# A hybrid decoder layer: carried state and decayed inputs in three rounded passes, z for two token blocks at a time

## The chip, the cores and the metric

The kernel runs on one core of a Trainium2 chip. The metric is the device time of one execution in microseconds (us); a single run reports it, and several runs are summed up by their median. A profile is of one further execution. Engines are named as the profile names them: PE multiplies matrices (PEld is its weight load), DVE is the vector engine, ACT the scalar engine with the transcendental functions, POOL the general engine, SP the one that issues most transfers.

## The reference

One layer: a half-weighted SwiGLU feed-forward block, a mixer, and a second feed-forward block, each followed by a residual and a layer norm, on 512 tokens of 1024 channels. The mixer adds a sliding-window attention and a state-space branch. The change lies in the state-space branch, cut here to what it computes for each of 4 groups of 8 heads, in 4 chunks of 128 tokens:

```python
proj = h @ w_in                      # z, xbc, dt, gates are column ranges of proj
xbc = silu(causal_depthwise_conv(xbc, conv_w, conv_b))        # gives x, B, C
CB = einsum("bclgn,bcsgn->bcgls", Cc, Bc)
y_diag = einsum("bcgls,bcgkls,bcsgkp->bclgkp", CB, Lmat, xdt)  # Lmat = exp of decay sums
states = einsum("bclgn,bcgkl,bclgkp->bcgkpn", Bc, decay_states, xdt)
...
# step over the chunks: h = chunk_decay * h + states ; prev is h before the step
y_off = einsum("bclgn,bcgkpn,bcgkl->bclgkp", Cc, prev, exp(A_cum))
...
u = (y_diag + y_off + d_skip * x) * silu(z)
u = u * rsqrt(mean(u * u, per group) + eps) * norm_w           # then u @ w_ssm_branch
```

## The kernel before, in words

All matrices are fp32, and nearly every product is made in three rounded passes. A value is split into a rounded high half and the rest (both of the type F32R): ACT casts the high half, DVE subtracts it from the value. `mm3` (L123 to L126) then issues high x high, high x rest and rest x high into one accumulator, as three matmuls with 512 moving columns (rows at L124, L125, L126). Weights come as 512 KB transfers on SP's queue into one of 3 `raw` buffers and are split by `split_w` into `wh` (ACT, L99) and `wl` (DVE, L100), 4 buffers each. Activations are split by `split_act` (ACT copy, then the DVE subtraction at L145). Two products of the state-space branch are not split but plain fp32 matmuls: `po`, C times the carried state `prev` (L615), and `pst`, B times the decayed inputs `xds` (L621). An fp32 matmul shows as two records, so that each line has 24 records for its 12 products.

The generator `ssd(g)` does one group. For a chunk c, `lead` lets POOL make four `ud` (L572); `decays` has PE sum them (L583, L584), ACT take exp of that (`seg`), DVE multiply `seg` twice by `cb`, itself from a PSUM product (L591, L593), DVE make `xdt` (L595) and POOL make `yx` (L597) and `xds` (L601). `products` has PE multiply `seg` by `xdt` (L609, 8 small products, 16 records), then `po` and `pst`; DVE adds these up into `yx`; POOL scales `prev` (L626), DVE adds `pst` to it. DVE then multiplies `yx` by `zs`, ACT takes the sum of squares, DVE scales it (`rs`, L633), POOL raises it to -1/2 (`rs`, L634), and DVE multiplies `yx` by it (L635). `turn(c)` has PE transpose the finished `yx` (L642, 4 blocks) for the next product. So from the end of a chunk's products to its `turn` there is a chain DVE, ACT, DVE, POOL, DVE, PE.

`weave` runs ssd(g), in ten steps, between large products ("mains"). First z of group 0, the convolution tiles (`xbc`) of group 1 and z of group 1 run beside ssd(0), whose ten steps fall on eight of the sixteen mains; then w_ssm of group 0 with the tiles and z of group 2 beside ssd(1); the same one further beside ssd(2); then w_ssm of group 2 and eight `gs_tile` beside ssd(3). In the profile ssd(0) takes about 621 to 723 us, ssd(1) 723 to 830, ssd(2) 830 to 918, ssd(3) 918 to 1027. `z_tiles` computes z of a group in four parts: each part loads one weight tile and multiplies it with all four token blocks, in four accumulators. A `gs_tile` makes a gate: a tanh to `tg`, a transfer of `tg` out and of `m1` in (POOL's queue), and two DVE operations on `ysum`.

The Tile framework places the instructions of this program on the engines; each engine then runs its own list strictly in that order, and waits at an instruction whose inputs or buffer are not there. PSUM has 8 banks here, 4 called `acc` for the large products and 4 called `sm` for the small ones.

Of the kernel before, what the change touches and what calls it, by code (L numbers as in the profile page):

```python
# [9 lines left out]
F32 = mybir.dt.float32  # L10
F32R = mybir.dt.float32r
# [3 lines left out]
P = 128  # L15
# [24 lines left out]
def hybrid_layer(  # L40
# [15 lines left out]
    def acc(name="acc"):  # L56
        return psum.tile([P, 512], F32, tag="acc", name=name)
# [230 lines left out]
    with tc.tile_pool(name="mix", bufs=1) as mix:  # L288
# [41 lines left out]
        def z_tiles(g, pool):  # L330

            pss = []

            def part(k2):
                if k2 == 0:
                    pss.extend(acc("z") for _ in range(NT))
                w2 = load_w(wcols(w_in, k2 * 256, 2, OFF_Z + g * 512, 512))
                for t in range(NT):
                    tok = slice(t * P, (t + 1) * P)
                    for j in range(2):  # L340
                        k = 2 * k2 + j
                        mm3(pss[t], xT[:, k, 0, tok], xT[:, k, 1, tok], w2[0][:, j], w2[1][:, j], k == 0, k == 7)
                if k2 < 3:
                    return
                for t in range(NT):
                    zs = pool.tile([P, 512], F32, name="zs", bufs=4)
                    nc.scalar.activation(zs, pss[t], AF.Tanh, scale=0.5)
                    nc.vector.scalar_tensor_tensor(zs, zs, 1.0, pss[t], ALU.add, ALU.mult)
                    cst["z", g, t] = zs

            return [lambda k2=k2: part(k2) for k2 in range(4)]
# [195 lines left out]
        with tc.tile_pool(name="ssd", bufs=1) as sp:  # L547
            ysum = sp.tile([P, 8, SEQ], F32, name="ysum")

            def ssd(g):  # L550
# [13 lines left out]
                st = [{} for _ in range(NT)]  # L564

# [11 lines left out]
                def decays(c):  # L577
# [20 lines left out]
                    xds = None  # L598
                    if c + 1 < NT:
                        xds = sp.tile([P, 512], F32, name="xds", bufs=1)  # L600
                        nc.gpsimd.tensor_tensor(hv(xds), hv(xdt), hb(dec[:, 1, c, hs]), ALU.mult)  # L601
                    st[c].update(segs=segs, xdt=xdt, yx=yx, xds=xds)

                def products(c):
# [7 lines left out]
                    if c > 0:  # L612
                        prev = st[c]["prev"]
                        po = sm()
                        nc.tensor.matmul(po, CT[:, tok], prev, start=True, stop=True)  # L615
# [3 lines left out]
                    if c + 1 < NT:  # L619
                        pst = sm()  # L620
                        nc.tensor.matmul(pst, Bn[:, c], xds, start=True, stop=True)  # L621
                        new = sp.tile([P, 512], F32, name="prev", bufs=2)
                        if c == 0:
                            nc.vector.tensor_copy(new, pst)
# [112 lines left out]
```

## Time and profile before

| quantity | value |
| --- | --- |
| time, median of 3 runs | 1453.4 us (1451.15 to 1454.14) |
| time of the profiled execution | 1453.2 us |
| span of the profiled execution | 1451.5 us |
| busy PE / DVE / ACT / POOL | 98% / 55% / 33% / 13% |
| granted PE clock, mean | 0.994 |

The span runs from the first to the last instruction that the profiler saw; 1.7 us of the execution lie around it. A busy share tells how long an engine had work in it. An engine that is busy nearly all the time is where the time is spent, unless its work is itself held up inside.

### The profile page before, as it was taken

Reading aid. Unit: us, or ns where it says so; the run is one execution under the profiler, and the core shown is the slowest. Engines: PE = TensorE matmul, PEld = TensorE weight load, DVE = VectorE, ACT = ScalarE, POOL = GpSimd, SP = SyncE. Lnnn points to the kernel's source line nnn. Section 1 sums busy time; section 2 is a strip of 40 time slices with the busy share of each in tenths; the row PEclk is TensorE's granted clock in tenths of the full one; section 3 lists DMA queues with packets and bytes.
Section 4 is the critical chain, followed back from the end, with each engine's and each line's share of the span. In section 5 each row is a group of like instructions: output and inputs, shape, how many; then the busy total and the mean of one; then the engine's idle time right before and its main releaser. Section 6 shows DMA issues by size and latency. Waiting matters only on the chain. (4 is left out here: it accounts for less than half of the span.)

```text
span 1451.5 us, 17121 instructions
## 1 busy us (share of the span) xinstructions
PE 1426.5 (98%) x6700; PEld 1169.7 (81%) x6700; DVE 791.5 (55%) x1246; ACT 482.1 (33%) x789; POOL 195.3 (13%) x214
## 2 busy tenths in 40 slices
PE   8999999999999999999999999999999999999997
PEld 6888888888877777887888888878878888888885
DVE  4343343233867884358659588686574434433235
ACT  4232232121346775223444234223313322322220
POOL 1000000000000000245244154261110000000001
PEclk9999999999999999999999999999999999999999
DMA  8433333323422133641231322345735333333321
GB/s 273 121 88 102 98 90 102 99 89 105 138 81 72 45 86 108 199 119 56 80 87 59 95 73 74 95 124 161 222 110 181 95 102 95 95 102 93 97 87 58
DMA packets 195633, 154.46 MB, mean 106 GB/s; under 512 B 6532, under 2 KB 169424, under 8 KB 195552
## 3 DMA queue, kind: packets, MB, share of 16 engines
q1 hardware_dynamic: 188608, 130.17, 30.1%
q0 software_dynamic: 6944, 23.19, 5.0%
q8 instruction: 53, 0.87, 0.3%
q14 instruction: 28, 0.23, 0.0%
HBM read 140.76 MB, written 12.58 MB: 106 GB/s over the span
## 5 line engine op out<-in xcount | busy, mean ns | idle before, releaser
L100 DVE TENSOR_TENSOR wl<-raw,wh 128x1024 fp32r<-128x1024 f32 (+1 forms) x233 | 299.6, 1287 | 417.3 <-ACT wh L99 412.6
L99 ACT CAST wh<-raw 128x1024 fp32r<-128x1024 f32 (+1 forms) x233 | 244.3, 1050 | 694.4 <-issue 323.7
L124 PE MATMUL acc<-xT,wh 128*128 128x512 f32 (+2 forms) x1120 | 441.9, 395 | 0.0
L125 PE MATMUL acc<-xT,wh 128*128 128x512 f32 (+2 forms) x1120 | 434.8, 388 | 0.0
L126 PE MATMUL acc<-xT,wl 128*128 128x512 f32 (+2 forms) x1120 | 433.8, 387 | 0.0
L124 PEld LDWEIGHTS acc<-xT,wh 128*128 128x128 f32 x1120 | 210.9, 188 | 44.5 <-issue 3.2
L125 PEld LDWEIGHTS acc<-xT,wh 128*128 128x128 f32 x1120 | 210.7, 188 | 44.2 <-issue 3.3
L126 PEld LDWEIGHTS acc<-xT,wl 128*128 128x128 f32 x1120 | 210.4, 188 | 43.0 <-issue 0.2
L124 PE MATMUL dn<-wh,hT 128*128 128x512 f32 x352 | 137.2, 390 | 0.0
L125 PE MATMUL dn<-wl,hT 128*128 128x512 f32 x352 | 137.1, 390 | 0.0
L126 PE MATMUL dn<-wh,hT 128*128 128x512 f32 x352 | 136.9, 389 | 0.0
L160 POOL TENSOR_TENSOR sts<-sts,cols 128x1 f32<-128x1 f32 x12 | 11.9, 990 | 719.9 <-DVE sts L159 719.9
L572 POOL TENSOR_TENSOR ud<-upper,dAr 128x512 fp32r<-128x512 f32 x64 | 86.4, 1378 | 104.2 <-PE sm L584 104.2
L239 DVE TENSOR_TENSOR t<-t,acc 128x512 f32<-128x512 f32 x44 | 30.2, 687 | 111.6 <-PE acc L126 111.4
L125 PEld LDWEIGHTS dn<-wl,hT 128*128 128x128 f32 x352 | 66.1, 188 | 13.7
L126 PEld LDWEIGHTS dn<-wh,hT 128*128 128x128 f32 x352 | 66.1, 188 | 13.6
L124 PEld LDWEIGHTS dn<-wh,hT 128*128 128x128 f32 x352 | 66.1, 188 | 13.6
L124 PE MATMUL z<-wh,xT 128*128 128x512 f32 x128 | 51.5, 402 | 0.0
L124 PE MATMUL acc<-uT,wh 128*128 128x512 f32 x128 | 50.5, 395 | 0.0
L126 PE MATMUL z<-wh,xT 128*128 128x512 f32 x128 | 49.9, 390 | 0.0
L125 PE MATMUL z<-wl,xT 128*128 128x512 f32 x128 | 49.9, 390 | 0.0
L126 PE MATMUL acc<-uT,wl 128*128 128x512 f32 x128 | 49.9, 390 | 0.0
(212 smaller groups left out, 1691.8 us busy)
## 6 DMA issues: line engine op xcount, KB each, us to landing
raw<-in_w_in_dram SPq DMA_DIRECT2D x66, 512.0 KB, 3.7
raw<-in_ffn_w_gate_dram SPq DMA_DIRECT2D x44, 512.0 KB, 3.8
raw<-in_ffn_w_up_dram SPq DMA_DIRECT2D x44, 512.0 KB, 3.7
raw<-in_ffn_w_down_dram SPq DMA_DIRECT2D x44, 512.0 KB, 3.6
raw<-in_w_ssm_branch_dram SPq DMA_DIRECT2D x16, 512.0 KB, 3.4
raw<-in_w_attn_branch_dram SPq DMA_DIRECT2D x8, 512.0 KB, 4.1
raw<-in_w_out_dram SPq DMA_DIRECT2D x8, 512.0 KB, 4.4
r<-in_x_dram SPq DMA_DIRECT2D x8, 256.0 KB, 5.7
```

The lines of the kernel that those rows point to most:

```text
L99: nc.scalar.copy(h[:, :n], raw[:, :n])
L100: nc.vector.tensor_tensor(l[:, :n], raw[:, :n], f(h[:, :n]), ALU.subtract)
L124: nc.tensor.matmul(ps, lh, rh, start=start, stop=False)
L125: nc.tensor.matmul(ps, lh, rl, start=False, stop=False)
L126: cur["mm"] = nc.tensor.matmul(ps, ll, rh, start=False, stop=stop)
L160: nc.gpsimd.tensor_tensor(mv[:, 3:4], mv[:, 2:3], mhalf[:, 0:1], ALU.pow)
L239: nc.vector.tensor_tensor(t, t, pu, ALU.mult)
L572: nc.gpsimd.tensor_tensor(ud[:, i], upper.unsqueeze(1).broadcast_to([P, 4, P]), f(dAr[:, i, c, h0:h0 + 4]).unsqueeze(2).broadcast_to([P, 4 ...
```

## The change

Three things change. First, `po` and `pst` go through `mm3`. Their operands are split by `split_act` into new tiles: `csp` (of C, 128 x 128) and `prs` (of `prev`, 128 x 512) for chunks 1 to 3, `bsp` (of B, 128 x 128) and `xds` (128 x 512, from POOL's product, now called `xd`) for chunks 0 to 2. All have one buffer. That makes 48 new ACT copies and 48 new DVE subtractions in all. `prev` is kept in one buffer and updated in place, so that POOL may scale it only after its split has been made. Second, `z_tiles` computes two token blocks at a time: parts 0 and 1 load two weight tiles each and do the first two blocks, parts 2 and 3 load none and do the other two with the same four tiles; two accumulators are in use at a time, and tanh and the DVE operation on the first two blocks come after part 1. Third, the `tg` and `m1` tiles of `gs_tile` are taken from the pools of `th` (2 buffers) and `ct` (3 buffers) instead of tiles with one buffer each.

```diff
--- before.py
+++ after.py
@@ -329,26 +329,28 @@
 
         def z_tiles(g, pool):
 
-            pss = []
-
-            def part(k2):
-                if k2 == 0:
-                    pss.extend(acc("z") for _ in range(NT))
-                w2 = load_w(wcols(w_in, k2 * 256, 2, OFF_Z + g * 512, 512))
-                for t in range(NT):
-                    tok = slice(t * P, (t + 1) * P)
-                    for j in range(2):
-                        k = 2 * k2 + j
-                        mm3(pss[t], xT[:, k, 0, tok], xT[:, k, 1, tok], w2[0][:, j], w2[1][:, j], k == 0, k == 7)
-                if k2 < 3:
+            ws, pss = [], []
+
+            def part(i):
+                pair, half = divmod(i, 2)
+                if pair == 0:
+                    ws.extend(load_w(wcols(w_in, k2 * 256, 2, OFF_Z + g * 512, 512)) for k2 in (2 * half, 2 * half + 1))
+                if half == 0:
+                    pss[:] = [acc("z") for _ in range(2)]
+                for k2 in (2 * half, 2 * half + 1):
+                    for j, ps in enumerate(pss):
+                        tok = slice((2 * pair + j) * P, (2 * pair + j + 1) * P)
+                        for k in (2 * k2, 2 * k2 + 1):
+                            mm3(ps, xT[:, k, 0, tok], xT[:, k, 1, tok], ws[k2][0][:, k % 2], ws[k2][1][:, k % 2], k == 0, k == 7)
+                if half == 0:
                     return
-                for t in range(NT):
+                for j, ps in enumerate(pss):
                     zs = pool.tile([P, 512], F32, name="zs", bufs=4)
-                    nc.scalar.activation(zs, pss[t], AF.Tanh, scale=0.5)
-                    nc.vector.scalar_tensor_tensor(zs, zs, 1.0, pss[t], ALU.add, ALU.mult)
-                    cst["z", g, t] = zs
-
-            return [lambda k2=k2: part(k2) for k2 in range(4)]
+                    nc.scalar.activation(zs, ps, AF.Tanh, scale=0.5)
+                    nc.vector.scalar_tensor_tensor(zs, zs, 1.0, ps, ALU.add, ALU.mult)
+                    cst["z", g, 2 * pair + j] = zs
+
+            return [lambda i=i: part(i) for i in range(4)]
 
         def xbc(g, pool):
             order = [4 * g + i for i in range(4)] + [16 + g, 20 + g]
@@ -562,6 +564,7 @@
                     return ap.rearrange("p (h d) -> p h d", h=HPG)
 
                 st = [{} for _ in range(NT)]
+                prev = []
 
                 def lead(c):
                     st[c]["ud"] = []
@@ -596,9 +599,18 @@
                     yx = sp.tile([P, 512], F32, name="yx", bufs=2)
                     nc.gpsimd.tensor_tensor(hv(yx), hv(xn[:, c]), hb(dB[:, hs]), ALU.mult)
                     xds = None
+                    if c > 0:
+                        csp = sp.tile([P, 2, P], F32R, name="csp", bufs=1)
+                        split_act((csp[:, 0], csp[:, 1]), CT[:, tok])
+                        st[c]["csp"] = csp
                     if c + 1 < NT:
-                        xds = sp.tile([P, 512], F32, name="xds", bufs=1)
-                        nc.gpsimd.tensor_tensor(hv(xds), hv(xdt), hb(dec[:, 1, c, hs]), ALU.mult)
+                        xd = sp.tile([P, 512], F32, name="xd", bufs=1)
+                        nc.gpsimd.tensor_tensor(hv(xd), hv(xdt), hb(dec[:, 1, c, hs]), ALU.mult)
+                        bsp = sp.tile([P, 2, P], F32R, name="bsp", bufs=1)
+                        split_act((bsp[:, 0], bsp[:, 1]), Bn[:, c])
+                        xds = sp.tile([P, 2, 512], F32R, name="xds", bufs=1)
+                        split_act((xds[:, 0], xds[:, 1]), xd)
+                        st[c]["bsp"] = bsp
                     st[c].update(segs=segs, xdt=xdt, yx=yx, xds=xds)
 
                 def products(c):
@@ -610,22 +622,25 @@
                                          start=True, stop=True)
                     nc.vector.tensor_tensor(yx, yx, py, ALU.add)
                     if c > 0:
-                        prev = st[c]["prev"]
+                        prs, csp = st[c]["prs"], st[c]["csp"]
                         po = sm()
-                        nc.tensor.matmul(po, CT[:, tok], prev, start=True, stop=True)
+                        mm3(po, csp[:, 0], csp[:, 1], prs[:, 0], prs[:, 1], True, True)
                         yo = sp.tile([P, 512], F32, name="yo", bufs=1)
                         nc.vector.tensor_tensor(hv(yo), hv(po), hb(dec[:, 0, c, hs]), ALU.mult)
                         nc.vector.tensor_tensor(yx, yx, yo, ALU.add)
                     if c + 1 < NT:
+                        bsp = st[c]["bsp"]
                         pst = sm()
-                        nc.tensor.matmul(pst, Bn[:, c], xds, start=True, stop=True)
-                        new = sp.tile([P, 512], F32, name="prev", bufs=2)
+                        mm3(pst, bsp[:, 0], bsp[:, 1], xds[:, 0], xds[:, 1], True, True)
                         if c == 0:
-                            nc.vector.tensor_copy(new, pst)
+                            prev.append(sp.tile([P, 512], F32, name="prev", bufs=1))
+                            nc.vector.tensor_copy(prev[0], pst)
                         else:
-                            nc.gpsimd.tensor_tensor(hv(new), hv(prev), hb(dec[:, 2, c, hs]), ALU.mult)
-                            nc.vector.tensor_tensor(new, new, pst, ALU.add)
-                        st[c + 1]["prev"] = new
+                            nc.gpsimd.tensor_tensor(hv(prev[0]), hv(prev[0]), hb(dec[:, 2, c, hs]), ALU.mult)
+                            nc.vector.tensor_tensor(prev[0], prev[0], pst, ALU.add)
+                        prs = sp.tile([P, 2, 512], F32R, name="prs", bufs=1)
+                        split_act((prs[:, 0], prs[:, 1]), prev[0])
+                        st[c + 1]["prs"] = prs
                     nc.vector.tensor_tensor(yx, yx, cst.pop(("z", g, c)), ALU.mult)
                     rs = sp.tile([P, P], F32, name="rs", bufs=2)
                     sq = sp.tile([P, 512], F32, name="yo", bufs=1)
@@ -673,10 +688,10 @@
 
             def gs_tile(j):
                 ps = gemm_T(load_w(wcols(w_in, 0, 8, OFF_GS + j * P, P)), xT, range(8))
-                tg = sp.tile([P, SEQ], F32, name="tg", bufs=1)
+                tg = mix.tile([P, SEQ], F32, name="th", bufs=2)
                 nc.scalar.activation(tg, ps, AF.Tanh, scale=0.5)
                 nc.gpsimd.dma_start(gsd[j], tg)
-                m1 = sp.tile([P, SEQ], F32, name="m1", bufs=1)
+                m1 = mix.tile([P, SEQ], F32, name="ct", bufs=3)
                 nc.gpsimd.dma_start(m1, m1d[j])
                 nc.vector.scalar_tensor_tensor(ysum[:, j], tg, 1.0, ysum[:, j], ALU.add, ALU.mult)
                 nc.vector.tensor_tensor(ysum[:, j], ysum[:, j], m1, ALU.add)
```

The framework's lists change with it. The lines of the kernel after are some 2 to 15 higher: L572 is L575, L597 is L600, L601 is L608 (`xds` is `xd`), L626 is L639, L634 is L649, L635 is L650.

On POOL, in the last two chunks of group 0: the `rs` (L634) of its second, third and fourth chunk (the only three `rs` here), among the `ud` of its own fourth chunk (the first `ud` row) and the `ud`, `yx` and `xds` of group 1. Before:

```order
L572 TENSOR_TENSOR ud<-upper,dAr 128x512 x4
L634 TENSOR_TENSOR rs<-rs,cols 128x1
L597 TENSOR_TENSOR yx<-xn,heads 128x512
L634 TENSOR_TENSOR rs<-rs,cols 128x1
L572 TENSOR_TENSOR ud<-upper,dAr 128x512 x4
L597 TENSOR_TENSOR yx<-xn,heads 128x512
L601 TENSOR_TENSOR xds<-xdt,dec 128x512
L634 TENSOR_TENSOR rs<-rs,cols 128x1
```

After:

```order
L575 TENSOR_TENSOR ud<-upper,dAr 128x512
L639 TENSOR_TENSOR prev<-prev,dec 128x512
L575 TENSOR_TENSOR ud<-upper,dAr 128x512 x3
L649 TENSOR_TENSOR rs<-rs,cols 128x1
L600 TENSOR_TENSOR yx<-xn,heads 128x512
L575 TENSOR_TENSOR ud<-upper,dAr 128x512 x4
L649 TENSOR_TENSOR rs<-rs,cols 128x1
L600 TENSOR_TENSOR yx<-xn,heads 128x512
L608 TENSOR_TENSOR xd<-xdt,dec 128x512 x2
L649 TENSOR_TENSOR rs<-rs,cols 128x1
```

The first `rs` still stands behind the fourth chunk's four `ud`, and now behind the scaling of `prev` of the chunk after its own as well; the second moved from before group 1's four `ud` to behind them; the last stood behind one `xds` of group 1 and stands behind two `xd`.

On POOL, from the fourth chunk of group 1 to its end. Before:

```order
L572 TENSOR_TENSOR ud<-upper,dAr 128x512 x4
L597 TENSOR_TENSOR yx<-xn,heads 128x512
L634 TENSOR_TENSOR rs<-rs,cols 128x1
L572 TENSOR_TENSOR ud<-upper,dAr 128x512 x4
L601 TENSOR_TENSOR xds<-xdt,dec 128x512
L597 TENSOR_TENSOR yx<-xn,heads 128x512
L634 TENSOR_TENSOR rs<-rs,cols 128x1
```

After:

```order
L575 TENSOR_TENSOR ud<-upper,dAr 128x512 x4
L600 TENSOR_TENSOR yx<-xn,heads 128x512
L575 TENSOR_TENSOR ud<-upper,dAr 128x512 x3
L649 TENSOR_TENSOR rs<-rs,cols 128x1
L575 TENSOR_TENSOR ud<-upper,dAr 128x512
L608 TENSOR_TENSOR xd<-xdt,dec 128x512
L600 TENSOR_TENSOR yx<-xn,heads 128x512
L608 TENSOR_TENSOR xd<-xdt,dec 128x512
L649 TENSOR_TENSOR rs<-rs,cols 128x1
```

The `rs` of the third chunk (the first here) moved from before the next group's `ud` to behind three of them, and a second `xd` came ahead of the last `rs`. Group 2 reads alike, with two `ud` in place of three.

On DVE, in the third chunk of group 3, from the product with `zs` of the second chunk to the `seg` products. Before:

```order
L629 TENSOR_TENSOR yx<-yx,zs 128x512
L633 TENSOR_SCALAR rs<-rs 128x1
L635 SCALAR_TENSOR_TENSOR yx<-yx,rs,normB 128x512
L100 TENSOR_TENSOR wl<-raw,wh 128x1024
L681 SCALAR_TENSOR_TENSOR ysum<-tg,ysum 128x512
L591 TENSOR_TENSOR cb<-sm,quarter 128x128
L682 TENSOR_TENSOR ysum<-ysum,m_7427 128x512
L593 TENSOR_TENSOR seg<-seg,cb 128x512 x2
```

After (the lines 644, 648, 650, 594 and 596 are the 629, 633, 635, 591 and 593 of before):

```order
L145 TENSOR_TENSOR prs<-prev,prs 128x512
L644 TENSOR_TENSOR yx<-yx,zs 128x512
L145 TENSOR_TENSOR bsp<-Bn,bsp 128x128
L145 TENSOR_TENSOR xds<-xd,xds 128x512
L598 TENSOR_TENSOR xdt<-xn,dth 128x512
L648 TENSOR_SCALAR rs<-rs 128x1
L696 SCALAR_TENSOR_TENSOR ysum<-th,ysum 128x512
L594 TENSOR_TENSOR cb<-sm,quarter 128x128
L650 SCALAR_TENSOR_TENSOR yx<-yx,rs,normB 128x512
L697 TENSOR_TENSOR ysum<-ysum,ct 128x512
L596 TENSOR_TENSOR seg<-seg,cb 128x512 x2
L100 TENSOR_TENSOR wl<-raw,wh 128x1024 x2
```

Four subtractions come in ahead of the `seg` products, and the weight split that stood ahead of them stands behind them.

## Rows read from the trace of the kernel before

**Rows 1.** Page, busy time of each engine (us, share of the span, instructions)

```profile
PE 1426.5 (98%) x6700; PEld 1169.7 (81%) x6700; DVE 791.5 (55%) x1246; ACT 482.1 (33%) x789; POOL 195.3 (13%) x214
```

**Rows 2.** Groups by line and shape, PE (busy us, mean ns | idle before)

```profile
L615 PE MATMUL sm<-prev,CT 128*128 128x512 f32 x24 | 14.5, 689 | 0.0
```

**Rows 3.** Timeline of PE, group 1, chunk 2 (start, us, instruction)

```profile
785.95 1.08 PE L615 MATMUL sm<-prev,CT 128*128 128x512 f32 x2
786.87 1.02 PE L621 MATMUL sm<-xds,Bn 128*128 128x512 f32 x2
787.32 0.79 PE L124 MATMUL acc<-xT,wh 128*128 128x512 f32 x1
787.95 0.40 PE L125 MATMUL acc<-xT,wh 128*128 128x512 f32 x1
```

**Rows 4.** Windows (us, then busy PE, PEld, DVE, ACT, POOL; clock; DMA share; GB/s)

```profile
620.80:723.00 102.20, 99.88 (x472) 80.44 (x471) 73.10 (x93) 37.52 (x58) 43.86 (x40) 0.98 0.28 82
...
680.10:683.40 3.30, 3.30 (x8) 1.50 (x6) 3.30 (x5) 1.58 (x3) 0.00 (x0) 0.50 0.24 68
...
970.30:973.60 3.30, 3.30 (x6) 1.40 (x5) 3.30 (x6) 0.00 (x0) 0.62 (x2) 0.50 0.76 255
```

**Rows 5.** Timeline of PE, rows with a wait (in brackets: idle before, releaser)

```profile
662.79 1.10 PE L609 MATMUL sm<-xdt,seg 128*128 128x64 f32 x8 [0.80 <-DVE seg L593]
...
677.78 1.10 PE L609 MATMUL sm<-xdt,seg 128*128 128x64 f32 x8 [0.54 <-DVE seg L593]
...
679.22 0.99 PE L609 MATMUL sm<-xdt,seg 128*128 128x64 f32 x7 [0.34 <-DVE seg L593]
...
709.40 0.63 PE L642 MATMUL sm<-ident,yx 128*128 128x128 f32 x4 [0.64 <-DVE yx L635]
...
968.09 2.00 PE L609 MATMUL sm<-xdt,seg 128*128 128x64 f32 x16 [1.16 <-DVE seg L593]
```

**Rows 6.** Groups by line and shape, DVE (busy us, mean ns | idle)

```profile
L145 DVE TENSOR_TENSOR hT<-t,hT 128x512 fp32r<-128x512 f32 x44 | 30.1, 685 | 0.0
...
L591 DVE TENSOR_TENSOR cb<-sm,quarter 128x128 f32<-128x128 f32 x16 | 4.5, 279 | 0.0
```

**Rows 7.** Timeline of POOL, groups 0 and 1

```profile
652.04 1.04 POOL L601 TENSOR_TENSOR xds<-xdt,dec 128x512 f32<-128x512 f32 x1 [3.87 <-PE sm L621]
...
670.09 5.08 POOL L572 TENSOR_TENSOR ud<-upper,dAr 128x512 fp32r<-128x512 f32 x4 [0.95 <-PE sm L584]
...
792.99 0.55 POOL L634 TENSOR_TENSOR rs<-rs,cols 128x1 f32<-128x1 f32 x1 [6.47 <-DVE rs L633]
794.37 4.93 POOL L572 TENSOR_TENSOR ud<-upper,dAr 128x512 fp32r<-128x512 f32 x4 [0.84 <-PE sm L584]
801.67 2.02 POOL L601 TENSOR_TENSOR xds<-xdt,dec 128x512 f32<-128x512 f32 x1 [2.36 <-DVE xdt L595]
```

**Rows 8.** Timeline of DVE, groups 0, 1 and 3

```profile
697.24 1.23 DVE L100 TENSOR_TENSOR wl<-raw,wh 128x1024 fp32r<-128x1024 f32 x1 [0.36 <-ACT wh L99]
...
796.88 0.74 DVE L305 SCALAR_TENSOR_TENSOR CT<-acc,cols,CT 128x509 f32<-128x509 f32 x1
...
808.29 0.75 DVE L635 SCALAR_TENSOR_TENSOR yx<-yx,rs,normB 128x512 f32<-128x512 f32 x1 [0.66 <-POOL rs L634]
...
962.48 2.06 DVE L100 TENSOR_TENSOR wl<-raw,wh 128x1024 fp32r<-128x1024 f32 x1
...
967.36 1.28 DVE L593 TENSOR_TENSOR seg<-seg,cb 128x512 f32<-128x512 f32 x2
```

**Rows 9.** Timeline of PE, group 1, chunk 3 and its end

```profile
801.16 1.90 PE L609 MATMUL sm<-xdt,seg 128*128 128x64 f32 x16
...
804.28 0.40 PE L126 MATMUL z<-wh,xT 128*128 128x512 f32 x1
...
809.07 0.40 PE L126 MATMUL z<-wh,xT 128*128 128x512 f32 x1
809.30 0.60 PE L642 MATMUL sm<-ident,yx 128*128 128x128 f32 x4
```

## The prediction

> **What bounds the kernel now.** First the busy time: PE works in 1426.5 of 1451.5 us [rows 1], so only work taken from PE, or a wait of PE taken away or put in, changes the time. Then the groups by line: the two plain fp32 products are 24 in all, with 24 records each [rows 2]. Then PE's own rows with a wait, in the stretch of the state-space branch (621 to 1027 us): they are few, between 0.3 and 1.2 us, and all come from DVE's `seg` or from the finished `yx` [rows 5]. Before PE's rows, last, the rows of POOL and DVE that feed them. The windows show two more losses there: 3.3 us at half clock in group 0 and again in group 3, right behind a wait, each of which does the work of half its length, so some 1.7 us are lost [rows 4].
>
> **The products.** The rounded passes start 21 passes apart at 804.28 and 809.07: 4.79 / 21 = 0.228 us each [rows 9]. A `po` and a `pst` next to each other start at 785.95, and the second rounded pass behind them at 787.95 [rows 3]. One pass taken off, two fp32 products take 787.95 - 0.23 - 785.95 = 1.77 us, 0.89 each. Three passes take 0.68, so 0.21 less; 24 products give **-5.0 us**. The first pass behind an fp32 product starts late (787.32 to 787.95 is 0.63 for one pass), and I count that as the fp32 product's cost. If it were not the product's but came with any change of operand, a new product would pay it again, and next to nothing would be won: the bounds of the term are -5.0 and 0. I take -5.0, since the passes of large products follow each other at 0.23 also where every pass loads other weights, as it would here.
>
> **The new splits.** 48 ACT copies lie on an engine that is busy 37.52 of 102.20 us in group 0 [rows 4] and cost nothing there by themselves. Of the 48 DVE subtractions, 24 are long, 0.69 us as the subtraction of the same shape in the feed-forward block, and 24 short, 0.28 as the 128 x 128 product [rows 6]: 23 us over four groups, 5.8 in each. DVE is busy 73.10 of 102.20 in group 0 [rows 4], so they fit into it; the time hangs on where they and the lists put the chain behind `seg` and `yx`. I go through the places where PE waits, or has little in hand.
>
> Group 3, chunk 2. PE waits 1.16 for `seg` at 968.09 [rows 5] because a weight split of 2.06 stands ahead of the `seg` products on DVE [rows 8]; the list after has it behind them. The new subtractions are ahead of them too, but they can run while DVE would wait for `rs`. I take the whole wait and half clock as gone: 1.3 (the wait and the lost start) + 1.7 = **-3.0**. If the half clock comes anyway it is -1.3.
>
> Group 0, chunk 1: the wait of 0.80 at 662.79 [rows 5] goes, since a weight split and an `xdt` leave the place ahead of `seg`, some 2.6, against 1.7 of new subtractions: **-0.8**.
>
> Group 0, chunk 2: the `rs` of chunk 1 stands behind four `ud` of 5.08 [rows 7], and now behind the scaling of `prev` too, a POOL product of the shape that takes 1.04 to 2.02 [rows 7]. So `turn` waits 1.2; the 0.54 at 677.78 and 0.34 at 679.22 [rows 5] go, since the first `seg` is now ahead of the last `yx` product: **+0.3**. The half clock there (680.1) I keep as it is.
>
> Group 0, chunk 3: `rs` of chunk 2 moves behind four `ud` (4.93 for four in group 1 [rows 7]) that themselves wait until PE has read the ones of chunk 3. DVE's `yx` product, and behind it `cb` and `seg`, wait as long. Before, there were some 4 us in hand: **+1.2**, with 0 to 2.5 as bounds.
>
> End of group 0: PE waits 0.64 already [rows 5]. The last `rs` now stands behind two `xd`; the second of them waits until the first has been split, 1.5 for the second `xd` and that split; a third weight split, 1.23 when alone [rows 8], stands ahead on DVE. Against that PE has 45 passes from `po` to `turn` in place of 39, 6 x 0.23 = 1.4. So 0.64 + 1.5 + 1.2 - 1.4 = 2.0, and **+1.5** with the 0.2 that PE comes earlier (the shorter `po`). Bounds 0 and 2.7, the latter if the 1.4 does not count.
>
> Group 1, chunk 3: `rs` of chunk 2, at 792.99 before the `ud`, moves behind three of them, which start at about 794.2 [rows 7]: 794.2 + 3 x 1.23 + 0.55 = 798.4, and with the `yx` product of 0.75, two operations of 0.74 and two `seg` of 0.64 each [rows 8] behind it the second `seg` is ready at 798.5 + 0.75 + 1.5 + 1.3 = 802.0, some 0.1 later with hand-overs. PE starts its products at 801.16 [rows 9], earlier in the changed kernel by what was won till then in this chunk, 0.4, and needs the second `seg` at half of them, 801.6: **+0.5**, and 0.3 more for two restarts, **+0.8**. Group 2 has two `ud` there and so 1.2 in hand: nothing.
>
> Ends of groups 1 and 2: `yx` is ready at 808.29 + 0.75 = 809.04 [rows 8], PE comes to `turn` at 809.30 [rows 9]: 0.26 in hand. Now `yx` waits for `rs` behind a second `xd`, which waits for an `xdt`, which on DVE stands behind the product of `yx` and `zs`: 0.2 + 0.6 later, if the `xd` takes 1.04, and 1.0 more if it takes 2.02 [rows 7]; PE comes 0.2 earlier. 0.8 + 0.2 - 0.26 = 0.74 each: **+1.5**.
>
> **The other two edits.** `z_tiles` issues the same passes from the same loads in the same order of transfers, and the four `zs` come two by two; four weight buffers are held longer, so the next load's split waits longer, but two raw tiles can lie ready. I count nothing; the bound is one late weight split per group, 1.2 x 4 = +5. The buffers of `gs_tile` give room in group 3 alone, where PE's one wait has been counted: nothing.
>
> **The sum.** -5.0 - 3.0 - 0.8 + 0.3 + 1.2 + 1.5 + 0.8 + 1.5 = -3.5. The profiled execution took 1453.2 us, 1.7 more than its span and 0.2 less than the median of the runs shown: 1449.7, and by the median some 0.2 more. I say **1449.8**.
>
> **Rivals.** *Nothing new waits.* The positive terms, 5.3 in all, stay out because POOL and DVE reach those steps earlier than I put them: 1449.8 - 5.3 = 1444.5. For it speaks that each is only 0.3 to 1.5 on chains of 5 to 10 us; against it that PE has only 0.26 in hand at two group ends and nothing at the third.
>
> *The passes win nothing* (the bound above): 1449.8 + 5.0 = 1454.8. For it, the 0.63 of the first pass after the fp32 products; against it, that no such step shows between large passes.
>
> *More half clock.* A wait of over 1 us was followed by half clock in group 3, and one of 0.54 and 0.34 in group 0 [rows 4, 5]. If two of the new waits bring one each, of 1.7: 1453.2.
>
> *DVE and POOL in each other's way: slower.* A weight split takes 2.06 in one place and 1.23 in another [rows 8], and POOL's `xds` 2.02 and 1.04 [rows 7]: the long ones lie beside work of the other engine, 0.8 to 1.0 extra each. The change puts 24 long subtractions on DVE, each with both its inputs in SBUF. If, at the six places with a wait above, both long subtractions (`prs` and `xds`) meet a POOL product, 12 x 0.9 = 10.8 more lie on the path: 1460.6. It is slower than before by over 2.9 from seven of the twelve on (7 x 0.9 = 6.3). For it, that POOL is busy 43.86 of 102.20 [rows 4], so four in ten would meet one by chance, which is five of the twelve; against it, that the subtractions wait for POOL's own `xd` and so start when it has ended. The Trainium skill, page "SBUF — State Buffer", section "Who interferes with whom", says that a DVE instruction with two SBUF inputs contends with a GpSimd instruction that reads SBUF, and that the one that comes second is held up for the whole of the other. The trace agrees with it in kind: 0.83 on a split and 0.98 on an `xds`, not whole instructions of the other. By the whole of the other, 1.23 for each `ud`, the rival would cost 12 x 1.23 = 14.8 instead.
>
> **Chances and range.** The forecast 0.42, its own range 1447.5 to 1452; nothing new waits 0.20; passes win nothing 0.08; more half clock 0.16; slower 0.14. What a measurement of this kernel can tell is about 0.2%, 2.9 us: faster is below 1450.5, slower above 1456.3. Faster takes all of the second and somewhat over half of the forecast's 0.42 (0.26), and little else: 0.47. Slower is the last rival, 0.14; the rest, 0.39, is the same. The range reaches from 1444.3, the case in which nothing waits, to 1456.0, which holds the two middle rivals and leaves the slower one out.
>
> **What would show it.** Right: in the profile after, `po` and `pst` are three records each, 0.23 apart, also from the last one to the next large product; the half clock at the third chunk of group 3 is gone and no wait for `seg` stands there; at the three `turn`s that end groups 0 to 2, PE waits for `yx` for 0.7 to 2 us, with `rs` on POOL directly behind an `xd`. Wrong: a gap of 0.4 at each change from a split product to a large one; those three waits missing, or long ones elsewhere; new stretches at half clock in the second row of the page; DVE's long subtractions of `prs` and `xds` at 1.2 or more on average; PE waiting for `acc` or a weight split within z, which I put at nothing.

## The result and the profile after

The changed kernel takes 1463.71 us (median of 4 runs, 1461.02 to 1465.16) against 1453.49 for the kernel before (4 runs, 1451.15 to 1454.14): ratio 1.0077, 95% interval 1.0064 to 1.0089. It is 10.2 us slower, 13.9 over the forecast of 1449.8 and outside the range.

The busy time of the changed kernel, for [rows 1]:

```profile
PE 1427.0 (98%) x6724; PEld 1177.7 (80%) x6724; DVE 810.5 (55%) x1294; ACT 501.7 (34%) x837; POOL 200.2 (14%) x214
```

DVE has 19 us more and ACT 20, and PE's busy time is that of before, though the span is 11.6 us longer. So PE waits, and longer than whatever the passes took off it. What PE waited for between 600 and 1050 us in the changed kernel (total us, times, longest):

```profile
PE sm L657 <- DVE yx L650: 9.9, 6, 3.7
PE sm L621 <- DVE seg L596: 3.6, 6, 1.2
PE sm L124 <- ACT xn L326: 0.3, 1, 0.3
```

The same question to the kernel before:

```profile
PE sm L609 <- DVE seg L593: 2.8, 4, 1.2
PE sm L642 <- DVE yx L635: 0.6, 1, 0.6
```

The finished `yx` went from 0.6 to 9.9 us, `seg` from 2.8 to 3.6. One step further back, what DVE waited for in its rescale of `yx`, before and (in the second fence) after, from 620 to 1040 us:

```profile
DVE yx L635 <- POOL rs L634: 11.3, 14, 2.5
```

```profile
DVE yx L650 <- POOL rs L649: 20.0, 15, 3.5
```

So `rs` on POOL is late. PE's rows with these waits in the changed kernel, for [rows 5]:

```profile
679.39 0.66 PE L657 MATMUL sm<-ident,yx 128*128 128x128 f32 x4 [1.10 <-DVE yx L650]
...
698.24 0.63 PE L657 MATMUL sm<-ident,yx 128*128 128x128 f32 x4 [1.43 <-DVE yx L650]
...
716.43 1.09 PE L657 MATMUL sm<-ident,yx 128*128 128x128 f32 x4 [3.69 <-DVE yx L650]
...
818.81 0.63 PE L657 MATMUL sm<-ident,yx 128*128 128x128 f32 x4 [0.92 <-DVE yx L650]
...
918.19 0.63 PE L657 MATMUL sm<-ident,yx 128*128 128x128 f32 x4 [2.58 <-DVE yx L650]
...
979.14 1.10 PE L621 MATMUL sm<-xdt,seg 128*128 128x64 f32 x8 [1.21 <-DVE seg L596]
981.30 1.71 PE L621 MATMUL sm<-xdt,seg 128*128 128x64 f32 x8 [1.06 <-DVE seg L596]
```

The first three are the `turn`s in chunks 2 and 3 and at the end of group 0, the next two the ends of groups 1 and 2, the last two group 3, chunk 2. From the first sum of `ud` to the last `turn`, PE takes 361.8 us (645.1 to 1006.9) against 352.4 (642.5 to 995.0): 9.4 longer. The rest of the span's 11.6 is this execution's: it comes to that stretch 2.6 later, nearly all of it (2.5) from the first 16 us, where both kernels are the same, and is 0.3 faster behind it.

### The profile page after: what moved, and what is told of

Read it like the earlier page. It is cut to its first block, busy times and chain, and to the rows that moved or that the text cites. A ratio compares the mean times of both kernels' runs of the same rounds, so it can differ in the third digit from the quotient of the medians.

```text
span 1463.1 us, 17251 instructions
## 1 busy us (share of the span) xinstructions
PE 1427.0 (98%) x6724; PEld 1177.7 (80%) x6724; DVE 810.5 (55%) x1294; ACT 501.7 (34%) x837; POOL 200.2 (14%) x214
## 5 line engine op out<-in xcount | busy, mean ns | idle before, releaser
L100 DVE TENSOR_TENSOR wl<-raw,wh 128x1024 fp32r<-128x1024 f32 (+1 forms) x233 | 289.9, 1246 | 406.8 <-ACT wh L99 406.1
L99 ACT CAST wh<-raw 128x1024 fp32r<-128x1024 f32 (+1 forms) x233 | 244.1, 1050 | 677.9 <-issue 318.5
L575 POOL TENSOR_TENSOR ud<-upper,dAr 128x512 fp32r<-128x512 f32 x64 | 87.5, 1394 | 106.3 <-PE sm L587 106.2
```

Source lines behind the costliest of these rows:

```text
L99: nc.scalar.copy(h[:, :n], raw[:, :n])
L100: nc.vector.tensor_tensor(l[:, :n], raw[:, :n], f(h[:, :n]), ALU.subtract)
L575: nc.gpsimd.tensor_tensor(ud[:, i], upper.unsqueeze(1).broadcast_to([P, 4, P]), f(dAr[:, i, c, h0:h0 + 4]).unsqueeze(2).broadcast_to([P, 4 ...
```

## The experiments

Theory A: the time goes into the order of the lists. `rs` and the rescale of `yx` stand behind POOL's and DVE's work for the next chunk or group. Rivals: the added work itself (B), the z edit (C), passes that win nothing (D). The kernel before had medians of 1451.3 to 1452.0 beside these runs; each ratio is to the runs of the kernel before on the same chip.

**The z edit alone, and its absence.** `z_only` is the kernel before with the new `z_tiles`; `z_old` the changed kernel with the old one.

> The kernel before with the z edit alone. Theory A (the loss is the order: the rs and yx rescale at a chunk's end queue behind POOL's and DVE's work for the next chunk or group, which the new splits bring in): POOL's list here is that of before, so no new wait of a turn, 1452.0 to 1455.0 us. Theory C (z in pairs of blocks holds four weight tiles and delays the splits and the zs at the group ends): most of the loss is here, over 1458 us, with PE waits at the ends of groups 0 to 2.

Measured: 1451.97 against 1452.02 of the kernel before, ratio 1.0002 (0.9993 to 1.0012).

> The changed kernel with z as it was before: rounded passes, splits and the two gate tiles moved. Theory A: the waits of PE for the finished yx stay, 1460 to 1465 us. Theory C: the loss is gone, 1448 to 1452 us.

Measured: 1463.91, ratio 1.0093 (1.0076 to 1.0111). The z edit makes no difference clear of the noise, some 1.5 us without the other two edits and 3.5 with them (4 runs); C, which put most of the loss on it, falls. What it changes is where PE waits, in `z_old`:

```profile
PE z L124 <- DVE CT L305: 6.2, 2, 3.2
PE sm L655 <- DVE yx L648: 4.4, 5, 1.4
PE sm L619 <- DVE seg L594: 2.9, 4, 1.2
```

The old z takes four accumulators at once, and waits until DVE has read the convolution's tile from one (L305); DVE is late because the rescale stands ahead of that read. PE pays earlier for the same lateness, and less at the `turn`.

**The order on POOL.** `issue_after` makes an engine issue what is traced inside it behind a given instruction of that engine; it adds no wait for data.

```diff
+                def behind(keys, fn, c):
+                    with ExitStack() as es:
+                        for k in keys:
+                            if ("rs", *k) in cst:
+                                es.enter_context(tc.issue_after(cst["rs", *k]))
+                        fn(c)
-                    nc.gpsimd.tensor_tensor(rs[:, 1:2], rs[:, 0:1], mhalf[:, 0:1], ALU.pow)
+                    cst["rs", g, c] = nc.gpsimd.tensor_tensor(rs[:, 1:2], rs[:, 0:1], mhalf[:, 0:1], ALU.pow).ins
-                lead(0)
+                behind([(g - 1, 2)], lead, 0)
-                        decays(c)
+                        behind([(g - 1, 3)] if c < 2 else [], decays, c)
-                            lead(c + 1)
+                            behind([(g, c - 1)], lead, c + 1)
```

> The changed kernel with an order on POOL: the ud of a chunk, and the yx and xd of the next group's first two chunks, are issued behind the rs of the last chunk but one (or the last one of the group before). Nothing else is taken away. Theory A: PE's waits for yx fall from 9.9 us to under 4, and the time to 1453 to 1458 us. Theory B (the 48 subtractions and 48 copies are too much work by themselves for DVE and ACT, wherever rs stands): the waits stay above 8 us and the time at 1461 to 1465.

Measured: 1452.21, ratio to the kernel before 1.0004 (0.9995 to 1.0014): 11.5 us less than the changed kernel (11.7 less than `z_old`, run beside it), with every split, copy and pass in it. DVE's wait for `rs` there, and PE's for `yx`:

```profile
DVE yx L657 <- POOL rs L656: 7.8, 15, 0.7
```

```profile
PE sm L664 <- DVE yx L657: 5.3, 4, 3.1
```

From 20.0 to 7.8 us, and none over 0.7. A holds and B falls, for all that the change had lost; 5.3 us of waits for `yx` are left, where A had under 4. The lists of DVE and ACT differ from the changed kernel's in little but the place of the `xds` split, which follows its `xd`.

Most of what is left is at the end of group 0: 3.13 of the 3.69. There `rs` now comes without an `xd` ahead of it and the sum of squares 0.1 behind `yx` times `zs`; but PE comes to the `turn` 0.2 us after that product and not 2.0, since the waits of the chunk before are gone. What comes last there is DVE's work up to that product; no run was made that takes it away.

**The passes without splits.**

```diff
-                        nc.tensor.matmul(po, CT[:, tok], prev, start=True, stop=True)
+                        mm3(po, xT[:, 0, 0, tok], xT[:, 0, 1, tok], prev, prev, True, True)
-                        nc.tensor.matmul(pst, Bn[:, c], xds, start=True, stop=True)
-                        new = sp.tile([P, 512], F32, name="prev", bufs=2)
+                        mm3(pst, xT[:, 2, 0, tok], xT[:, 2, 1, tok], xds, xds, True, True)
+                        new = sp.tile([P, 512], F32R, name="prev", bufs=2)
```

(Not shown: `xds` is F32R as well, written so by POOL, and two lines read `prev` as F32. This kernel leaves out the low halves of both moving operands, and has slices of the layer's activations in place of C and B, so that its outputs differ.)

> The kernel before with both products in three passes, but no splits: the moving operand is the state or the decayed input rounded once and used in all three passes, the fixed one a slice of the activations, so the outputs lack the low halves and the B and C. Theory A: PE gains about 24 x 0.17 = 4 us; POOL's list has the rs of three chunks behind three ud, which may give back up to 3: 1449 to 1453 us, with no wait over 1.5 us at the ends of groups 0 to 2. Theory D (three passes cost as much as the fp32 products): 1453 us or more, with the passes themselves over 0.85 us a product.

Measured: 1458.62, ratio 1.0055 (1.0040 to 1.0070). Not one split is in this kernel, and 6.6 of the 10.2 us are there. POOL's rows of group 1, chunk 3 show why:

```profile
794.16 4.02 POOL L572 TENSOR_TENSOR ud<-upper,dAr 128x512 fp32r<-128x512 f32 x3 [7.49 <-PE sm L584]
798.14 0.54 POOL L634 TENSOR_TENSOR rs<-rs,cols 128x1 f32<-128x1 f32 x1
```

DVE's, and then PE's there:

```profile
798.72 1.52 DVE L635 SCALAR_TENSOR_TENSOR yx<-yx,rs,normB 128x512 f32<-128x512 f32 x1 [2.52 <-POOL rs L634]
800.17 0.73 DVE L305 SCALAR_TENSOR_TENSOR CT<-acc,cols,CT 128x510 f32<-128x510 f32 x1
```

```profile
802.31 0.47 PE L124 MATMUL z<-wh,xT 128*128 128x512 f32 x1 [3.21 <-DVE CT L305]
```

`rs` stands behind three `ud`, DVE waits for it with two reads of the convolution behind, and z waits for those. [Rows 7] show the same `rs` at 792.99, ahead of the `ud`. DVE's list has a part in it too: a weight split, itself waiting for ACT, now stands ahead of DVE's scaling of `rs`, so that POOL could not have begun before 795.3:

```profile
794.06 1.23 DVE L100 TENSOR_TENSOR wl<-raw,wh 128x1024 fp32r<-128x1024 f32 x1 [2.00 <-ACT wh L99]
795.20 0.15 DVE L633 TENSOR_SCALAR rs<-rs 128x1 f32<-128x1 f32 x1
```

My expectation gave this up to 3 us and missed.

**The order with and without the passes.** The edit of the order above, in the kernel before and in the passes without splits; their POOL lists are then alike. They differ by the products, and by DVE's and ACT's lists: that weight split stays ahead of `rs` in the second.

> The kernel before with the same order on POOL as the run before this (rs ahead of the ud of the chunk after next, and of the next group's first products). In the kernel before only the ends of the groups and one chunk of group 0 change by it. Theory A: PE's wait of 0.64 at the end of group 0 goes and little else, 1449.5 to 1453.5 us: the order is no gain of its own, only something that the change took away. Rival E (the order is worth as much here as in the changed kernel): 1446 us or less.

Measured: 1451.74, ratio 0.9996 (0.9987 to 1.0006): no gain of its own. I expected the wait of 0.64 at the end of group 0 to go; it grew to 1.68, and 0.51 came at the ends of groups 1 and 2.

> The three passes without splits (as in the run of that kind before: one rounding, outputs without the low halves) and with the order on POOL; POOL's list is then that of the kernel before with the order, and the two differ by the products alone. Theory A: the loss of 6.6 us of the passes without the order was the rs behind three ud; it goes, and the passes show their 24 x 0.17: 1446 to 1450 us, 3 to 5 under the kernel before with the order. Theory D (three passes win nothing): within 1 us of that kernel.

Measured: 1451.91, ratio 0.9996 (0.9987 to 1.0005). The loss of 6.6 us is gone, as A says, but the passes won nothing over 1451.74. Beside the waits for `yx` (2.9 us) stood waits of z for the accumulators, in this run:

```profile
PE z L124 <- DVE CT L305: 3.8, 3, 1.4
```

**The splits without the passes**, with the order on POOL.

```diff
-                        mm3(po, csp[:, 0], csp[:, 1], prs[:, 0], prs[:, 1], True, True)
+                        nc.tensor.matmul(po, CT[:, tok], prev[0], start=True, stop=True)
-                        mm3(pst, bsp[:, 0], bsp[:, 1], xds[:, 0], xds[:, 1], True, True)
+                        nc.tensor.matmul(pst, Bn[:, c], st[c]["xd"], start=True, stop=True)
```

> The changed kernel with the order on POOL and all 48 casts and subtractions, but the products plain fp32 of the unsplit values: the splits are made and not used. Theory A: the splits cost what the waits at the ends of the groups cost with the order (some 4 to 6 us), and PE's 4 us are lost too: 1454 to 1458 us. Theory B' (the splits are hidden where the order is right): 1450 to 1453 us.

Measured: 1453.02, ratio to before 1.0011 (1.0000 to 1.0021). All 96 split operations, with the z edit and the gate tiles, cost 1.3 us (0 to 2.6) over the kernel before with the order (1451.74), so most of their work is hidden where the order is right: 0.02 us over what B' had. The run with the passes in their place has 1452.21, on another chip; 0.8 is within the noise of such a pair.

**The order on DVE too**: the next group's first two chunks on DVE behind the last rescale.

```diff
-                        behind([("rs", g - 1, 3)] if c < 2 else [], decays, c)
+                        behind([("rs", g - 1, 3), ("yr", g - 1, 3)] if c < 2 else [], decays, c)
-                    nc.vector.scalar_tensor_tensor(yx, yx, rs[:, 1:2], normB, ALU.mult, ALU.mult)
+                    cst["yr", g, c] = nc.vector.scalar_tensor_tensor(yx, yx, rs[:, 1:2], normB, ALU.mult, ALU.mult).ins
```

> The changed kernel with the order on POOL and one on DVE: the next group's first two chunks (xdt, cb, seg and the splits) are issued behind the last rescale of yx of the group before. The waits of PE for yx at the three group ends were 3.5, 1.4 and 1.4 us with POOL's order alone. Theory A (what is left is the next group's DVE work ahead of rs): they fall to 1.5, 0.5 and 0.5 or less, 1446 to 1450 us. Theory B (the amount of DVE work, wherever it stands): no change, 1451 to 1453 us.

Measured: 1450.53, ratio 0.9986 (0.9976 to 0.9997), between A and B. In the traces, the waits fell from 0.96 and 1.00 to 0.41 and 0.45 at the ends of groups 1 and 2, and stayed at that of group 0 (3.13, now 3.10); the 3.5, 1.4 and 1.4 of the expectation are higher than the trace has them. At the end of group 1, DVE's rescale and POOL's `rs` and next `yx` in this run:

```profile
809.24 1.52 DVE L657 SCALAR_TENSOR_TENSOR yx<-yx,rs,normB 128x512 f32<-128x512 f32 x1 [0.66 <-POOL rs L656]
```

```profile
808.66 0.55 POOL L656 TENSOR_TENSOR rs<-rs,cols 128x1 f32<-128x1 f32 x1 [5.90 <-DVE rs L655]
809.17 1.04 POOL L607 TENSOR_TENSOR yx<-xn,heads 128x512 f32<-128x512 f32 x1
```

**POOL out of the rescale's way.**

```diff
-                        behind([("rs", g - 1, 3), ("yr", g - 1, 3)] if c < 2 else [], decays, c)
+                        behind([("rs", g - 1, 3), ("yr", g - 1, 3), ("nb", g)] if c < 2 else [], decays, c)
```

(`cst["nb", g]` is the transfer that loads `normB`, which has to wait for the rescale that reads the old one)

> The changed kernel with the orders on POOL and DVE, and POOL's yx and xd for the next group behind its own load of normB, which waits for the last rescale of yx. In the run without this the rescale took 1.52 where POOL's yx began beside it, and 0.75 where nothing did. Theory G (a DVE operation of two SBUF inputs is held up by the POOL product beside it, and this is on the path at three group ends): the rescale takes 0.75, PE's waits there fall from 3.3, 0.6 and 0.6 us to 2.5 and 0, the time to 1447.5 to 1449.5 us. Rival H (the length of the rescale is not what PE waits for): the waits and the time stay, 1449.8 to 1451.5 us.

Measured: 1448.42, ratio to before 0.9975 (0.9966 to 0.9984): faster than both kernels. The rescale at the end of group 1, and PE's waits:

```profile
806.45 0.75 DVE L657 SCALAR_TENSOR_TENSOR yx<-yx,rs,normB 128x512 f32<-128x512 f32 x1 [0.66 <-POOL rs L656]
```

```profile
PE sm L664 <- DVE yx L657: 2.5, 2, 2.3
PE sm L628 <- DVE seg L603: 1.0, 3, 0.4
PE sm L125 <- DVE xds L145: 1.0, 1, 1.0
```

The rescale takes 0.75 in place of 1.52, the waits at the ends of groups 1 and 2 are gone, and that of group 0 fell from 3.10 to 2.32. DVE's and ACT's lists are those of the run before, and only POOL's changed, so G holds. How much of the time this step alone is worth is less sure: the two runs were on two chips, and the intervals of their ratios overlap.

**What the passes and z are worth with the order.** Three kernels put together from the edits above: the passes without splits with POOL's order and the new z; the changed kernel with POOL's order and the old z; the kernel before with all three orders (the first and the third without the gate tiles' edit).

> The three passes without splits (one rounding, outputs without the low halves), with the order on POOL and now with z in pairs of blocks. Without the z edit this kernel was no faster than the kernel before with the order, and its PE waited 5.0 us where z takes its four accumulators while DVE still reads a convolution tile from one. Theory F (the passes do win some 4 us of PE, and z given all four accumulators at once hands them back): these waits go and the time falls to 1447 to 1449.5 us. Theory D (three passes win nothing): 1451 to 1453 us.

Measured: 1450.41, ratio 0.9990 (0.9981 to 1.0000): between F and D. The waits for the accumulators went (3.8 us in the trace without the z edit, not 5.0), but those for `yx` grew from 2.9 to 4.9 us.

> The changed kernel with the order on POOL and z as it was before. With z in pairs it took 1452.2 us. Theory F (z with four accumulators waits for the convolution's last reads on DVE when PE comes early or DVE late): waits of z for the accumulator of 4 to 7 us, 1454 to 1459 us. Theory C' (how z is tiled does not matter): 1451 to 1453.5 us.

Measured: 1451.93, ratio 1.0002 (0.9993 to 1.0011); with z in pairs it was 1452.21. The waits of z came (3.9 us), those for `yx` fell from 5.3 to 2.8. F is right on the place of the wait and wrong on the time. But the equal times hide a difference: the granted clock was 0.997 in most of these runs and 0.995 in most of the others, and at the same clock (0.995, 0.996, 0.997) these are 0.8 to 2.0 us longer, on few runs. So z in pairs moves the wait and may win a little by itself; these runs do not settle it.

> The kernel before with all three orders (rs ahead on POOL, the last rescale ahead of the next group on DVE, POOL's next yx behind the load of normB). Theory A (these orders only undo what the change brought, and take the one wait of 0.6 at the end of group 0): 1449.5 to 1452 us, so that the changed kernel with the same orders is 1.5 to 4 us faster than this one. Rival E: 1447 us or less, and the changed kernel wins nothing over it.

Measured: 1450.13, ratio 0.9991 (0.9982 to 1.0000). With equal orders the change as a whole wins 1.7 us (1450.13 to 1448.42), and not by the clock: at 0.995 and 0.996 the runs of the changed kernel are 1.9 and 2.4 us shorter.

## Why the prediction was wrong

I had -3.5 for this stretch, and it took 9.4 more: 12.9 off. Of these, 4.3 lie at the end of group 0, 4.2 in group 3's chunk 2, 2.4 at the ends of groups 1 and 2, 1.6 in group 0's chunk 3 and 0.9 in the products; the rest nearly cancels. The direction was right at each place but group 3's chunk 2 and group 0's chunk 2; the sizes failed. Below, what a place cost is how far the same product of PE slid against the kernel before between that place's ends, with the products' own gain put back.

**The products: right in kind, -4.1 in place of -5.0.** The changed kernel's rows, for [rows 3]:

```profile
793.82 0.48 PE L124 MATMUL sm<-prs,csp 128*128 128x512 f32 x1
794.14 0.39 PE L125 MATMUL sm<-prs,csp 128*128 128x512 f32 x1
...
795.53 0.39 PE L125 MATMUL acc<-xT,wh 128*128 128x512 f32 x1
```

By the same measure two products take 795.53 - 0.23 - 793.82 = 1.48, 0.74 each against 0.89, 0.15 less; 24 give 3.5. That ends at the second pass behind them. By how far the products further on moved up, the 14 products that lie clear of any wait win 2.42 us, 0.17 each, and 24 give 4.1. The first pass costs 0.32 and not 0.23. The gap of 0.63 after an fp32 product went with it, so the rival in which the passes win nothing was wrong on PE's rows. In the kernel's time less is left: nothing without splits (1451.74 to 1451.91) and 1.7 us for the change as a whole with all orders, since PE, come earlier, waits longer for the chain.

**Group 3, chunk 2: a step that failed, +1.2 in place of -3.0.** The weight split did go behind the `seg` products. I took the four subtractions ahead of them as time that DVE would have waited anyway, and the two `seg` at 1.28, as before. On DVE, rows of the changed kernel:

```profile
970.36 1.13 DVE L145 TENSOR_TENSOR bsp<-Bn,bsp 128x128 fp32r<-128x128 f32 x1
971.42 0.68 DVE L145 TENSOR_TENSOR xds<-xd,xds 128x512 fp32r<-128x512 f32 x1
972.02 1.52 DVE L598 TENSOR_TENSOR xdt<-xn,dth 128x512 f32<-128x512 f32 x1
...
974.67 1.52 DVE L650 SCALAR_TENSOR_TENSOR yx<-yx,rs,normB 128x512 f32<-128x512 f32 x1 [0.26 <-POOL rs L649]
976.11 1.52 DVE L697 TENSOR_TENSOR ysum<-ysum,ct 128x512 f32<-128x512 f32 x1
977.56 3.69 DVE L596 TENSOR_TENSOR seg<-seg,cb 128x512 f32<-128x512 f32 x2
```

and on POOL beside them:

```profile
974.61 3.93 POOL L575 TENSOR_TENSOR ud<-upper,dAr 128x512 fp32r<-128x512 f32 x3
```

Counted from PE's first sum for this chunk (959.71 before, 970.71 after), the scaling of `rs` on DVE comes 2.3 us later than before, behind two of the subtractions and an `xdt`. So POOL's `rs` is late, and its last three `ud` run when DVE comes to the rescale, `ysum` and `seg`. The two `seg` begin 0.8 us earlier than before by that count, but take 3.69 us where [rows 8] have 1.28, and end 1.6 later. Half clock stayed too, 0.50 from 982.8 to 984.9.

**The end of group 0: the other step that failed, +3.0 of wait, and 2.7 at half clock behind it, in place of +1.5.** Rows of the changed kernel on POOL, ACT and DVE:

```profile
710.26 2.23 POOL L608 TENSOR_TENSOR xd<-xdt,dec 128x512 f32<-128x512 f32 x1 [5.88 <-DVE xdt L598]
713.95 1.04 POOL L608 TENSOR_TENSOR xd<-xdt,dec 128x512 f32<-128x512 f32 x1 [1.46 <-DVE rs L648]
714.95 0.55 POOL L649 TENSOR_TENSOR rs<-rs,cols 128x1 f32<-128x1 f32 x1
```

```profile
712.52 0.62 ACT L144 CAST xds<-xd 128x512 fp32r<-128x512 f32 x1 [3.16 <-POOL xd L608]
713.05 0.63 ACT L647 ACTIVATE yo<-yx 128x512 f32<-128x512 f32 x1
```

```profile
710.09 0.69 DVE L644 TENSOR_TENSOR yx<-yx,zs 128x512 f32<-128x512 f32 x1
...
713.17 0.69 DVE L145 TENSOR_TENSOR xds<-xd,xds 128x512 fp32r<-128x512 f32 x1 [1.59 <-ACT xds L144]
713.80 0.15 DVE L648 TENSOR_SCALAR rs<-rs 128x1 f32<-128x1 f32 x1
715.53 0.75 DVE L650 SCALAR_TENSOR_TENSOR yx<-yx,rs,normB 128x512 f32<-128x512 f32 x1 [1.58 <-POOL rs L649]
```

`yx` times `zs` is done at 710.8. The step that I had as "1.5 for the second `xd` and that split" left out the first `xd` and a third list: ACT's sum of squares stands behind ACT's copy for the split of the next group's `xds`, and that behind POOL's `xd`, which took 2.23 beside DVE. The sum of squares could start at 710.8 and starts at 713.05; then the second `xd` adds 1.04. I had read POOL's and DVE's lists and not ACT's. PE waits 3.69 in place of 0.64; the `turn` slides by 4.4, but 1.4 of that are the six passes of z that come ahead of it and not behind. The passes behind the `turn` then run at half clock, which the sum had at nothing.

**The other ends and third chunks.** Group 1's end cost 1.1 (forecast 0.74), group 2's 2.8. There DVE's way from `po` to `rs` was longer by 2.0, with `bsp`, `xds` and one operation at 1.51 in place of 0.68, and POOL's by 0.7, an `xd`. DVE came to it late, too: the rescale of chunk 2 had waited 2.20 for an `rs` behind two `ud`, which I had put at nothing:

```profile
904.00 1.52 DVE L650 SCALAR_TENSOR_TENSOR yx<-yx,rs,normB 128x512 f32<-128x512 f32 x1 [2.20 <-POOL rs L649]
```

Group 1's chunk 3 cost 1.0 (forecast 0.8), group 0's 2.8 (1.2), where four `ud` took 6.5, against 4.9 and 5.1 in [rows 7]. Chunk 1 of group 0 gave 0.4 (0.8), and chunk 2 gave 1.3 where I had a loss of 0.3: PE waited 1.10 there, as forecast (1.2), but the half clock of [rows 4] did not come. All terms together: -4.1 - 0.4 - 1.3 + 2.8 + 5.8 + 1.0 + 1.1 + 0.3 (group 2's chunk 3) + 2.8 + 1.2 + 0.2 (group 3's chunk 3) = 9.4.

**The slower rival** came nearest in time (1460.6), but by luck: it named the long subtractions, and they are not held up. Their rows in the changed kernel, 620 to 1030 us (busy us, mean ns):

```profile
L145 DVE TENSOR_TENSOR prs<-prev,prs 128x512 fp32r<-128x512 f32 x12 | 8.2, 684 | 0.0
L145 DVE TENSOR_TENSOR xds<-xd,xds 128x512 fp32r<-128x512 f32 x12 | 8.2, 681 | 1.6 <-ACT xds L144 1.6
```

The operations that got longer here were others: the mean of `xdt` rose from 945 to 1289 ns, of the rescale from 799 to 1041 and of `seg` from 1036 to 1106. (The rival's count was one short: seven of the twelve give 1456.1, and slower began at 1456.3.) That I gave "no new wait" 0.20 and the waits one size each was the fault of the range: with POOL's order pinned nearly all of them shrank at once.

**What is argued and not shown.** That the lists differ because the framework places POOL's work by when it thinks PE and the inputs are ready fits the passes without splits, whose program differs from the kernel before by the products and two tile types, and whose list has `rs` behind three `ud`. How it decides was not tried. No run has the edit of the gate tiles alone; it is in every kernel here that has both splits and the new `prev`, and it may have a part in group 3. Why half clock came at one place and went at another is open.

## What to carry to other kernels

Where a scheduler writes the engines' lists, a change that saves time on the busiest engine can move a short instruction of the chain that releases it behind long ones that are ready sooner: compare the lists of every engine on that chain, ACT's too, and pin the short one ahead. The edits here cost 10 us in the order that the framework gave them, and were worth 1.7 where both kernels had the orders pinned. If two tilings of the consumer differ only in where it waits, look for what is late behind both.

## What the hardware showed

The rescale of `yx` takes 0.75 us alone and 1.52 when a POOL product has begun 0.07 before it: 0.77 more, three quarters of that product's 1.04, which itself did not get longer. This agrees nearly with the Trainium skill, page "SBUF — State Buffer", section "Who interferes with whom", by which the instruction that comes second stands until the other is done: the rescale would end at 810.21 + 0.75 = 810.96, and ends at 810.76.

One can stand behind several. In the fastest version, three POOL products follow each other from 808.12 to 811.16, and a subtraction of 128 x 128 on DVE that begins 0.20 after the first takes 3.01 us, where the one for `csp`, of the same size, takes 0.28 at 910.03:

```profile
808.32 3.01 DVE L145 TENSOR_TENSOR bsp<-Bn,bsp 128x128 fp32r<-128x128 f32 x1
```

A wait of PE was not followed by half clock each time. Behind the one of 3.69 the granted clock was that of this window of the changed kernel (us, busy PE, PEld, DVE, ACT, POOL, clock):

```profile
718.00:721.60 3.60, 3.60 (x11) 2.83 (x10) 1.67 (x3) 1.62 (x4) 0.65 (x1) 0.50 0.24 71
```

Behind the one of 2.32 at the same place in the fastest version it stayed at full:

```profile
709.00:714.00 5.00, 5.00 (x27) 4.23 (x26) 5.00 (x5) 2.88 (x6) 3.51 (x4) 1.00 0.18 56
```

Group 3's wait of 1.16 before the change was followed by it [rows 4, 5]; so the length of the last wait alone does not tell.
